# A gated MLP on one core: the first products taken per block of 128 tokens as each is turned, the second weight in two loads of whole rows, one sum of x in a tile of its own

## The chip, the cores and the metric

The kernel runs on one core of a Trainium2 chip. The metric is the device time of one execution in microseconds (us), the median of several runs. Below, PE is the matrix engine (a weight load and a matmul are two instructions of it), DVE, ACT and POOL are the vector, scalar and GpSimd engines, SP is the engine that only issues transfers here. Each engine works through its own queue in order; semaphores tie the queues together.

## The reference

```python
batch, seq, dim, hidden = 16, 256, 512, 2048   # x, w1 (dim x 2*hidden), w2 (hidden x dim), float32
h = x @ w1
gate, value = np.split(h, 2, axis=-1)
h = np.maximum(gate, 0) * value
return (h @ w2).astype(np.float32)
```

So there are 4096 tokens of 512 numbers; the first product makes 2 x 2048 numbers of each (a gate and a value), the second brings 2048 back to 512.

## The kernel before

**Tiling.** The tokens go in four sweeps `s` of 1024, each two halves of 512. A sweep has 16 hidden blocks `jb` of 128; after the last one, the second product of the sweep runs as a stream of 128 steps that interleaves with the next sweep's first blocks. Both products take seven multiplications where a plain 2 x 2 block product takes eight. For the first one the 2 x 2 blocks of x are A11, A12 (first half of the tokens, first and second 256 of dim) and A21, A22 (second half); those of w1 are B11, B12, B21, B22 (rows of dim by gate and value). Sums T1..T4 of weight blocks (T1 = B12 - B11, T2 = B22 - T1, T3 = B22 - B12, T4 = B21 - T2) and S1..S4 of x blocks (S1 = A21 + A22, S2 = S1 - A11, S4 = A12 - S2, S3 = A11 - A21) are made first. A block's seven products are called P1 (B11, A11), P2 (B21, A12), P3 (B22, S4), P4 (T4, A22), P5 (T1, S1), P6 (T2, S2), P7 (T3, S3); each is two matmuls of 512 columns, 14 in all. Between them ACT copies X to Y after P1 (L252; P2 waits for it, since it adds into X), makes scaled copies after P5 and P6 (L259, L266), and DVE joins the parts (L272, L273, L278, L288). The second product does the same with g (the gated result) and w2: its sums are L165 on g (into `w_stage`) and T1..T4 on w2's tiles (`vop`).

**The weights' way in.** w1 arrives in nine pieces `wl`: hidden blocks 0 and 1 alone, then seven pairs (2,3) .. (14,15). A load of a piece is two transfers on SP's queue, gate columns and value columns (L212, 256 KB each for the single blocks, in rows of 512 bytes; 512 KB each for the pairs), into six slots of `w_stage`; a slot is loaded again only when ACT has copied its B11, B21, B22 (L231, `copy_some`) and POOL has made its T1..T4 (L227, `sum_w1`). The fifth piece (blocks 6, 7) goes into the slots of blocks 0 and 1, the sixth (8, 9) into those of (2, 3). w2 arrives by POOL's own queue, in float16, in four transfers of 512 KB (L668), each issued between two pieces' sums. When the last piece is done, POOL issues the casts of x for the next sweeps (L192) and then makes w2's T1 and T2 (L670, L671, 128 x 2048 each).

**The start.** The T's need both halves of a piece, and S's need the second half of the tokens, so hidden blocks 0 and 1 of sweep 0 are computed by the plain way, eight products (`Plain`, L314): a gate and a value, each four matmuls, per token half. x arrives in eight blocks of 128 tokens (L475) and is turned by PE (L485; the first four from float32, the last four from float16 after a cast by POOL or DVE, L478), DVE and ACT copying the turned halves out of PSUM (L488). Fillers that compute nothing (`arm`, `keep_busy`, L502 and L150) stand between. The order of every engine's queue is the order in which the code is written: SP first x blocks 0 and 1, the gate columns of w1's block 0, x blocks 2 and 3, its value columns, both transfers of block 1, then x blocks 4 to 7 and the first pairs. PE: x blocks 0 and 1 turned; fillers; block 0's gate on 256 tokens; x blocks 2 and 3 turned; fillers; its gate on the other 256; its value; block 1's gate and value; then x blocks 4 to 7 turned among the same for the second half. Copies of block 0's and 1's weights to float16 (`plain_w`): three on POOL (L455), one on ACT (L456). The seven-product blocks begin with block 2; its P1 stands before the last piece of block 1's value.

**The second product's sums.** `SUMS_FIRST` and the lines under `if s == 0` say at which step of the stream DVE is given each sum; an emission at step u stands in DVE's queue before what step u itself gives it. In `SUMS_FIRST` each bracket is a token block t with the steps of its S1, S2, S4, S3.

Of the kernel before, what the change touches and what calls it, by code (L numbers as in the profile page):

```python
# [96 lines left out]
def fast_way(ctx, tc, x2, w1, w2, out2, flag):  # L97
# [27 lines left out]


    w1_v = w1.rearrange("(e p) (g j) -> g p e j", p=P, g=2)
    w2_v = w2.rearrange("(u hc p) (v n) -> u v p hc n", u=2, v=2, p=P)
    out_v = out2.rearrange("(s h b p) n -> s h b p n", p=P, h=2, b=NB // 2)

    wop = {n: wpool.tile([P, 2, H], F16, name=f"w_{n}") for n in ("B11", "B21", "B22", "T1", "T2", "T3", "T4")}
    vop = {n: wpool.tile([P, NJ // 2, DO // 2], F16, name=f"v_{n}") for n in ("B11", "B21", "B22", "T1", "T2", "T3", "T4")}
    w_stage = wpool.tile([P, 6, 1024], F32, name="w_stage")
    g_set = {0: gpool.tile([P, NJ, 2 * TH], F16, name="g", tag="g")}

# [11 lines left out]
    def keep_busy(n):  # L147

        for _ in range(n):
            nc.tensor.matmul(Y[:, :TH // 2], warm_b[:, :P], warm_b[:, :TH // 2], start=False, stop=True,  # L150
                             skip_group_check=True)
# [29 lines left out]
    def look_whole(t, at, of, half=False):  # L181

        sq = tmp.tile([P, 1024], F16, name="sq", tag="sq", bufs=1)
        nc.scalar.activation(sq[:, :of], t, SQUARE, scale=(P / of / (2 if half else 1)) ** 0.5,
                             accum_out=st[:, at:at + 1])

    x16 = {}
# [21 lines left out]
    def load_w1(eng, jb, n, u, vs=(0, 1)):  # L209
        t = w_stage[:, u:u + n].rearrange("p u v -> p (u v)").rearrange("p (g e j) -> p g e j", g=2, e=4)  # L210
        for v in vs:
            eng.dma_start(out=t[:, v], in_=w1_v[v, :, :, jb * P:(jb + n) * P])  # L212
        return t.rearrange("p g (k b) j -> p k b g j", k=2)
# [23 lines left out]

    class Block:
        def __init__(self, xo, g, jb):
            self.xo, self.g, self.jb = xo, g, jb  # L240

        def mm(self, name, ps, fresh):
            wn, xn = WX[name]
# [24 lines left out]
        def P3(self):  # L268
            self.mm("P3", self.W, False)
            cc = tmp.tile([P, 2, TH], F32, name="cc", tag="tmp")  # L270
            self.c12, self.c22 = cc[:, 0], cc[:, 1]
            nc.vector.scalar_tensor_tensor(out=self.c12, in0=self.W, scalar=GS, in1=self.u2, op0=MULT, op1=ADD)  # L272
            nc.vector.scalar_tensor_tensor(out=self.g[:, self.jb, :TH], in0=self.X, scalar=0.0,  # L273
                                           in1=self.c12, op0=MAX, op1=MULT)

        def P7(self):
            self.mm("P7", self.Y, False)
            nc.vector.scalar_tensor_tensor(out=self.c22, in0=self.Y, scalar=GS, in1=self.p5, op0=MULT, op1=ADD)  # L278
            second_halves()

        def P4(self):
# [11 lines left out]
    def second_halves():  # L293

        while later:
            later.pop(0).second_half()
# [129 lines left out]
    def fetch(i, eng):  # L426
        if i < len(wl):
            assert all(j > i - 3 for j, _ in copies)
            jb, n, u = wl[i]
            ws[i] = load_w1(eng, jb, n, u)  # L430
# [16 lines left out]
            c()  # L447
        del copies[:n]

    def plain_w(i):  # L450
        jb, n, _ = wl[i]
        t = ws.pop(i)
        js = slice(jb * P, (jb + n) * P)
        for n, k, v in (("B11", 0, 0), ("B21", 1, 0), ("T3", 0, 1)):
            nc.gpsimd.tensor_copy(out=wop[n][:, :, js], in_=t[:, k, :, v])  # L455
        return lambda: nc.scalar.copy(out=wop["B22"][:, :, js], in_=t[:, 1, :, 1])  # L456

    def plain_w_end(jb, n, i):
        n2, i0, i1 = (("T1", "T3", "B11"), ("T2", "B22", "T1"), ("T3", "B22", "T3"), ("T4", "B21", "T2"))[i]
# [17 lines left out]
    def cast_first(b, copy):  # L477
        copy(out=x16_first[b // 2][:, b % 2], in_=xn[1][b])  # L478
# [15 lines left out]
    def new_w():  # L494
        return psw.tile([P, TH], F32, name="W", tag="W")
# [4 lines left out]
    def arm(ps):  # L500

        nc.tensor.matmul(ps, warm_b[:, :P], warm_b[:, :TH], start=True, stop=True)  # L502

    dve, act, pool = nc.vector.tensor_copy, nc.scalar.copy, nc.gpsimd.tensor_copy
    fetch_first(0, (0, 1))
    ws[0] = load_w1(nc.sync, *wl[0], (0,))
    fetch_first(0, (2, 3))
    load_w1(nc.sync, *wl[0], (1,))
    fetch(1, nc.sync)
    make_identity(nc, ident)  # L510
    fetch_first(1, range(4))
    fetch(2, nc.sync)
# [4 lines left out]
    first_half, second_half = (xo["A11"], xo["A12"]), (xo["A21"], xo["A22"])  # L517
    YS = [new_y(), new_y()]

    def halves(*ts):  # L520
        return [t[:, :2 * P] for t in ts]

    def turns(t):
        return [t.bitcast(F16)[:, c:c + 2 * P] for c in (0, 2 * P)]

    rest = plain_w(0)
    turn_first(xo, 0, 0, halves(*YS), (dve, act))
    XS = [new_x(), new_x()]
    turn_first(xo, 0, 1, halves(*XS), (dve, act))
    arm(YS[0])  # L530
    arm(YS[1])
    keep_busy(3)
    plain[0].open(W=False)
    plain[0].part("gate", *first_half, half)
    turn_first(xo, 0, 2, halves(*XS), (dve, act))
    turn_first(xo, 0, 3, halves(new_w(), new_w()), (dve, act))
    keep_busy(2)
    plain[0].part("gate", *first_half, other)
    plain[0].W = new_w()
    rest()  # L540
    rest = plain_w(1)
    plain[0].part("value", *first_half)
    plain[0].value()
    plain[1].open()
    plain[1].part("gate", *first_half)
    rest()
    fetch(4, nc.sync)
    plain[0].gate(0)
    plain[1].part("value", *first_half)
    spare = plain[0].X, plain[1].W  # L550
    cast_first(0, pool)
    cast_first(1, dve)
    cast_first(2, pool)
    turn_first(xo, 1, 0, (turns(YS[0])[0], turns(YS[1])[0]), (dve, act))
    turn_first(xo, 1, 1, (turns(plain[0].X)[0], turns(plain[0].W)[0]), (dve, act))
    plain[1].value()
    held = plain[1].held(0)
    cast_first(3, dve)
    xo["S3"] = halfs.tile([P, 8, P], F16, name="xh", tag="xh").rearrange("p (a b) c -> p a (b c)", a=2)
    sums = [sums_of({n: t[:, :, slice(*c)] for n, t in xo.items()}) for c in (half, other)]  # L560
    next(sums[0])
    plain[0].open()
    plain[0].part("gate", *second_half, half)
    turn_first(xo, 1, 2, turns(spare[0]), (act, act))
    turn_first(xo, 1, 3, turns(spare[1]), (dve, dve))
    plain[0].part("value", *second_half, half)
    plain[1].open(*reversed(YS))
    plain[1].part("gate", *second_half, half)
    plain[1].part("value", *second_half, half)
    next(sums[1])  # L570
    next(sums[0])
    next(sums[1])
    plain[0].part("gate", *second_half, other)
    plain[0].part("value", *second_half, other)
    for n in ("S4", "S3"):
        sum_of(xo, n)
    held()
    prepare(2, False)
    sum_w1(6)
    copy_some(1)  # L580
    plain[0].value()
    copy_some(1)
    plain[1].part("gate", *second_half, other, False)
    prepare(3, False)
    w_sums[:4] = [w_sums[i] for i in (2, 0, 3, 1)]
    sum_w1()
# [5 lines left out]

    def last_plain_out():
        plain[1].value()
        plain[0].gate(1)
        plain[1].gate(1)

    LOOKX, looks = {}, []

# [11 lines left out]

    def look_w2(i):
        n = ("B11", "B21", "B22", "T1")[i // 2]
        look_whole(vop[n].rearrange("p (u h) n -> p u (h n)", u=2)[:, i % 2], NX + 16 + i, 1024, n == "T1")

    def judge():
        n = st.shape[1]
# [23 lines left out]
    TAIL = 4  # L641
    CASTS = {(0, 11): 1, (0, 14): 2, (1, 8): 3, (2, 3): 0}
    SUMS = (10, 11, 12, 13)
    SUMS_FIRST = (10, 11, 13, 45), (17, 22, 26, 53), (33, 37, 41, 66), (67, 72, 76, 80)
    SUMS_AT = (10, 11, 13, 15), (22, 26, 30, 36), (46, 53, 57, 61), (70, 78, 82, 87)
    for s in range(NS):
        if s not in g_set:
# [8 lines left out]
        for at in range(first * PERIOD, (NJ - 1) * PERIOD + 14):  # L656
# [3 lines left out]
            if at in plan:  # L660
                jb, n = plan[at]
                if s == 0 and n == "P5" and jb % 2 == 0:
                    todo += 1
                    if todo < len(wl):
                        prepare(todo)
                    if 5 <= todo < 9:
                        n2 = ("B11", "T3", "B22", "B21")[todo - 5]
                        nc.gpsimd.dma_start(out=vop[n2], in_=w2_v[(0, 0, 1, 1)[todo - 5], (0, 1, 1, 0)[todo - 5]])  # L668
                if (s, n, jb) == (0, "P7", 13):
                    nc.gpsimd.tensor_tensor(vop["T1"], vop["T3"], vop["B11"], op=SUB)  # L670
                    nc.gpsimd.tensor_tensor(vop["T2"], vop["B22"], vop["T1"], op=SUB)  # L671
                if n == "P1" and jb == (14 if s == 0 else 2) and s + 1 < NS:
                    xo_next = x_tiles()
                    load_x(s + 1, xo_next)
# [12 lines left out]
                if s == 0 and (n, jb) == ("P5", NPLAIN):  # L687
                    last_plain_out()
                if n == "P7" or (n, jb) == ("P5", NPLAIN + 1) or n == "P6" and (s, jb) != (0, NPLAIN):
                    copy_some(1)  # L690
                if s == 0 and n == "P7" and jb % 2:
                    fetch(jb // 2 + 5, nc.sync)
                if n == "P6" and (s, jb) in LOOKX:
# [12 lines left out]
            for u in at:  # L706
                job(u, lambda sums=sums: next(sums))
        if s == 0:
            for n2, i0, i1, at in (("T3", "B22", "T3", (46, 50)), ("T4", "B21", "T2", (57, 64))):
                for i, u in enumerate(at):  # L710
                    part = [vop[n][:, i * NJ // 4:(i + 1) * NJ // 4] for n in (n2, i0, i1)]
                    job(u, lambda part=part: nc.vector.tensor_tensor(*part, op=SUB))
            for i, u in enumerate((74, 78, 82, 83)):
                job(u, lambda i=i: plain_w_end(0, NPLAIN, i))
        if s + 1 < NS:
# [16 lines left out]
            job(90, lambda: tc.mark_branch_hint_location("general", "LikelyTaken", [ENG.PE, ENG.DVE, ENG.SP]))  # L732
            advance(stream, 112, jobs)
        prev = stream
    return verdict[1]
# [1 line left out]
_INS = ['x', 'w1', 'w2']  # L737
_OUTS = [((16, 256, 512), 'float32')]
# [25 lines left out]
```

## Time and profile before

| | us |
|---|---|
| median of 5 runs (310.17 to 311.2) | 310.22 |
| the profiled execution | 310.39 |
| its span in the trace | 308.6 |
| PE busy | 301.5 (98%), 1863 matmuls |
| DVE / ACT / POOL busy | 236.0 / 176.8 / 154.5 |
| granted TensorE clock, each of 40 slices | 0.9 or more of full |

The span is what the trace covers; 1.8 us lie around it. Busy times are shares of the whole span and say little of any one stage. A busy PE is counted up to a matmul's modelled end, which lies after the start of the next one; starts are the sharper reading. Where 512-column matmuls follow each other without a wait, two of them start 0.43 us after the two before (0.216 us each), and eight of 256 columns take 0.87 us (0.109 each): a start later than that is a wait, even where the busy time shows none.

### The profile page before, as it was taken

To read this page: it belongs to the slowest core of one execution; us is meant where nothing else is said; L and a number is where in the kernel's file an instruction comes from. 1 tells how busy PE (TensorE), PEld (TensorE's weight loads), DVE (VectorE), ACT (ScalarE), POOL (GpSimd) and SP (SyncE) were. 2 spreads that over 40 slices of the span, in tenths; PEclk is the share of its full clock that TensorE was granted. 3 is DMA by queue.
4 is the path that set the end of the run, shared out by engine and by line. 5 is a ranking of instruction groups with operands and counts; after the bars stand their busy time and mean duration, and the time that the engine had idled before them with its cause. 6 is when DMAs were issued, how large, how long until landed. Compare 5 with 4: busy or idle time off the path is not lost.

```text
span 308.6 us, 5215 instructions
## 1 busy us (share of the span) xinstructions
PE 301.5 (98%) x1863; PEld 181.6 (59%) x1863; DVE 236.0 (76%) x383; ACT 176.8 (57%) x350; POOL 154.5 (50%) x192
## 2 busy tenths in 40 slices
PE   7999999999999999999999999999999999999994
PEld 4554444588854444478864444458884444447883
DVE  1589888889778888887538888888536888888841
ACT  2588985445865555537855555545866555553231
POOL 1389999930058999400028968910006998700000
PEclk9999999999999999999999999999999999999999
DMA  6985798984684233001356910000325110001132
GB/s 201 353 264 189 225 233 105 166 182 80 207 255 100 73 69 68 2 0 36 136 179 112 189 66 4 0 0 4 134 101 173 35 36 0 1 3 34 53 118 74
DMA packets 37917, 32.87 MB, mean 106 GB/s; under 512 B 14465, under 2 KB 33409, under 8 KB 37761
## 3 DMA queue, kind: packets, MB, share of 16 engines
q1 hardware_dynamic: 33536, 26.22, 28.1%
q0 software_dynamic: 4352, 6.29, 12.0%
q8 instruction: 15, 0.25, 0.3%
q14 instruction: 14, 0.11, 0.1%
HBM read 27.26 MB, written 12.58 MB: 129 GB/s over the span
## 4 chain that ended last, share of the span: by engine, by line
PE 88%; DMA 6%; POOL 3%; DVE 1%; SPq 1%; issue 1%; ACT 0%; DVEq 0%; POOLq 0%
PE Y L245 24%; PE X L245 16%; PE W L245 16%; PE Y L351 14%; PE W L351 9%; PE X L351 8%; DMA w_stage<-in_w_dram 6%; POOL w_T L227 3%; SPq L475 1%; DVE w_stage L165 1%; DVE g L288 0%; ACT Y L252 0%; SPq L212 0%; ACT o L394 0%; PE X L630 0%
## 5 line engine op out<-in xcount | busy, mean ns | idle before, releaser
L245 PEld LDWEIGHTS <-w_T 128*128 128x128 f16 x496 | 48.5, 98 | 56.8 <-POOL w_T L227 0.3
L175 POOL TENSOR_TENSOR fold<-xh 128x1024 f32<-128x1024 f16 x16 | 30.3, 1894 | 92.3 <-DMA xh<-x 91.5
L245 PE MATMUL X<-x_A,w_B 128*128 128x512 f16 x248 | 73.7, 379 | 0.1
L245 PE MATMUL Y<-x_S,w_T 128*128 128x512 f16 x220 | 65.4, 379 | 0.0
L245 PEld LDWEIGHTS <-w_B 128*128 128x128 f16 x372 | 36.4, 98 | 42.4 <-issue 0.9
L272 DVE SCALAR_TENSOR_TENSOR cc<-W,pu 128x512 f32<-128x512 f32 x62 | 42.8, 691 | 20.3 <-ACT pu L266 20.3
L252 ACT COPY Y<-X 128x512 f32<-128x512 f32 x62 | 35.4, 570 | 38.0 <-PE X L245 37.7
L266 ACT ACTIVATE pu<-Y 128x512 f32<-128x512 f32 x62 | 37.0, 597 | 33.8 <-PE Y L245 32.8
L178 POOL TENSOR_TENSOR fold<-fold 128x512 f32<-128x512 f32 (+2 forms) x96 | 51.7, 539 | 7.5
L351 PEld LDWEIGHTS <-w_stage 128*128 128x128 f16 x512 | 49.8, 98 | 6.6 <-DVE w_stage L165 0.8
L278 DVE SCALAR_TENSOR_TENSOR cc<-Y,pu 128x512 f32<-128x512 f32 x62 | 42.8, 691 | 6.7
L273 DVE SCALAR_TENSOR_TENSOR g<-X,cc 128x512 f16<-128x512 f32 x62 | 42.9, 691 | 2.3
L288 DVE SCALAR_TENSOR_TENSOR g<-Y,cc 128x512 f16<-128x512 f32 x62 | 42.2, 681 | 1.8 <-PE Y L245 1.8
L351 PEld LDWEIGHTS <-g 128*128 128x128 f16 x384 | 37.6, 98 | 8.2
L259 ACT ACTIVATE pu<-W 128x512 f32<-128x512 f32 x62 | 37.2, 599 | 0.2 <-ACT Y L252 0.2
L245 PE MATMUL W<-x_S,w_B 128*128 128x512 f16 x124 | 36.9, 379 | 0.0
L245 PE MATMUL W<-x_S,w_T 128*128 128x512 f16 x124 | 36.9, 379 | 0.0
L245 PE MATMUL Y<-x_A,w_T 128*128 128x512 f16 x124 | 36.9, 379 | 0.0
L351 PE MATMUL Y<-v_T,w_stage 128*128 128x256 f16 x256 | 33.2, 273 | 0.0
L351 PE MATMUL X<-v_B,g 128*128 128x256 f16 x256 | 31.9, 273 | 0.0
L165 DVE TENSOR_TENSOR w_stage<-g 128x1024 f16<-128x1024 f16 x32 | 22.2, 710 | 0.2
L383 DVE SCALAR_TENSOR_TENSOR o<-W,pu 128x256 f32<-128x256 f32 x16 | 6.7, 422 | 18.4 <-PE W L351 18.4
(103 smaller groups left out, 289.5 us busy)
## 6 DMA issues: line engine op xcount, KB each, us to landing
w_stage<-in_w_dram SPq DMA_DIRECT2D x14, 512.0 KB, 5.9
out_dram<-o SPq DMA_DIRECT2D x26, 256.0 KB, 2.0
x<-in_x_dram POOLq DMA_DIRECT2D x4, 1024.0 KB, 9.2
xh<-x SPq DMA_DIRECT2D x16, 256.0 KB, 3.4
v_B<-in_w_dram POOLq DMA_DIRECT2D x3, 512.0 KB, 6.4
out_dram<-o SPq DMA_DIRECT2D x12, 128.0 KB, 1.7
w_stage<-in_w_dram SPq DMA_DIRECT2D x4, 256.0 KB, 6.0
x_S<-in_x_dram SPq DMA_DIRECT2D x4, 256.0 KB, 5.9
```

What stands on the lines that cost most here:

```text
L165: eng.tensor_tensor(o[n], o[i0], o[i1], op=op)
L175: nc.gpsimd.tensor_tensor(fold, t, t, op=MULT)
L178: nc.gpsimd.tensor_tensor(fold[:, :, :m], fold[:, :, :m], fold[:, :, m:2 * m], op=ADD)
L245: nc.tensor.matmul(ps, wop[wn][:, b, self.jb * P:(self.jb + 1) * P], self.xo[xn][:, b, :], start=fresh and b == 0, stop=b == 1, skip_group ...
L252: nc.scalar.copy(out=self.Y, in_=self.X)
L259: nc.scalar.activation(self.p5, self.W, COPY, scale=GS)
L266: nc.scalar.activation(self.u2, self.Y, COPY, scale=GS)
L272: nc.vector.scalar_tensor_tensor(out=self.c12, in0=self.W, scalar=GS, in1=self.u2, op0=MULT, op1=ADD)
L273: nc.vector.scalar_tensor_tensor(out=self.g[:, self.jb, :TH], in0=self.X, scalar=0.0, in1=self.c12, op0=MAX, op1=MULT)
L278: nc.vector.scalar_tensor_tensor(out=self.c22, in0=self.Y, scalar=GS, in1=self.p5, op0=MULT, op1=ADD)
L288: nc.vector.scalar_tensor_tensor(out=self.g[:, self.jb, TH:], in0=self.Y, scalar=0.0, in1=self.c22, op0=MAX, op1=MULT)
L351: nc.tensor.matmul(ps, self.op[an][:, i], vop[wn][:, i], start=name in ("P1", "P5") and i == 0, stop=i == NJ // 2 - 1, skip_group_check=True)
```

## The change

- SP's queue: both transfers of w1's block 0 stand before x blocks 2 and 3, both of block 1 behind them.
- `plain_w` takes one transfer at a time: its first matrix is copied by POOL, its second by DVE; ACT has none.
- Block 0's gate and value on the first 256 tokens come as soon as they can, and then both for x block 2 and for x block 3 alone (matmuls of 128 columns); block 0's second half does so for each of its four x blocks. Block 1 stays at 512 and 256 columns. Fillers are five, as before, and lie elsewhere. x block 4 is cast by DVE, 5 to 7 by POOL.
- S3 of sweep 0 lies in the tile `sq` (the scratch of ACT's later look at the weights) and no longer in a third `xh` buffer; the sums of the first 256 tokens and the last 256 are each made over 256 columns, S4 over all.
- In the seven-product block 2, DVE makes block 1's last g and block 2's own first g (`behind`) after P7's part and no longer before.
- At P6 of block 5 ACT no longer copies if the copy would be of the sixth w1 piece (8, 9); that copy comes one place later.
- w2 comes in two transfers of 1024 KB (whole rows: 512 numbers in place of 256), issued when the seventh and eighth pieces' sums are made, and the four former `vop` tiles are views of two row tiles.
- w2's T2: first half on POOL, second half on DVE at step 12. T4's second half at step 62 (64 before), S3 of t = 2 at step 64 (66 before).
- `look_w2` reads its piece as 4 x 256 and no longer as one row of 1024; the last value returned is `verdict[-1]`.

```diff
-    vop = {n: wpool.tile([P, NJ // 2, DO // 2], F16, name=f"v_{n}") for n in ("B11", "B21", "B22", "T1", "T2", "T3", "T4")}
+    vop = {n: wpool.tile([P, NJ // 2, DO // 2], F16, name=f"v_{n}") for n in ("T1", "T2", "T4")}
+    w2_rows = [wpool.tile([P, NJ // 2, DO], F16, name=f"w2_{u}") for u in range(2)]
+    vop.update({n: w2_rows[u][:, :, v * DO // 2:(v + 1) * DO // 2]
+                for n, u, v in (("B11", 0, 0), ("T3", 0, 1), ("B21", 1, 0), ("B22", 1, 1))})
...
+            if not self.behind:
+                self.first_half()
+
+        def first_half(self):
             nc.vector.scalar_tensor_tensor(out=self.g[:, self.jb, :TH], in0=self.X, scalar=0.0,
                                            in1=self.c12, op0=MAX, op1=MULT)
...
+            for job in self.behind:
+                job()
             second_halves()
...
+    def plain_w(i, v, engines):
+
+        (jb, n, _), t = wl[i], first_w[i]
         js = slice(jb * P, (jb + n) * P)
+        for k, (n, copy) in enumerate(zip((("B11", "B21"), ("T3", "B22"))[v], engines)):
+            copy(out=wop[n][:, :, js], in_=t[:, k, :, v])
+
+    def sum_w2(eng, n2, i0, i1, i):
+        eng.tensor_tensor(*[vop[n][:, i * NJ // 4:(i + 1) * NJ // 4] for n in (n2, i0, i1)], op=SUB)
...
     fetch_first(0, (0, 1))
-    ws[0] = load_w1(nc.sync, *wl[0], (0,))
+    first_w = [load_w1(nc.sync, *wl[0])]
     fetch_first(0, (2, 3))
-    load_w1(nc.sync, *wl[0], (1,))
-    fetch(1, nc.sync)
+    first_w.append(load_w1(nc.sync, *wl[1]))
...
+    plain_w(0, 0, (pool, dve))
     arm(YS[0])
     arm(YS[1])
+    plain[0].open()
+    plain[0].part("gate", *first_half, cols(0, 2))
+    plain_w(0, 1, (pool, dve))
+    keep_busy(4)
+    plain[0].part("value", *first_half, cols(0, 2))
+    turn_first(xo, 0, 2, halves(*XS, c=2 * P), (dve, act))
+    keep_busy(1)
+    turn_first(xo, 0, 3, halves(*YS, c=2 * P), (dve, act))
+    plain_w(1, 0, (pool, dve))
+    plain_w(1, 1, (pool, dve))
+    for b in (2, 3):
+        for which in ("gate", "value"):
+            plain[0].part(which, *first_half, cols(b), False)
+    fetch(4, nc.sync)
     plain[0].value()
     plain[1].open()
     plain[1].part("gate", *first_half)
+    cast_first(0, dve)
+    cast_first(1, pool)
+    cast_first(2, pool)
+    cast_first(3, pool)
+    plain[1].part("value", *first_half, half)
+    turn_first(xo, 1, 0, (turns(YS[0])[0], turns(YS[1])[0]), (dve, act))
     plain[0].gate(0)
+    plain[1].part("value", *first_half, other, False)
...
+    for which in ("gate", "value"):
+        plain[0].part(which, *second_half, cols(0))
+    turn_first(xo, 1, 1, (turns(YS[0])[1], turns(YS[1])[1]), (dve, act))
+    turn_first(xo, 1, 2, (turns(spare[0])[0], turns(spare[1])[0]), (dve, act))
+    xo["S3"] = tmp.tile([P, 1024], F16, name="sq", tag="sq", bufs=1).rearrange("p (a b) -> p a b", a=2)
...
+    turn_first(xo, 1, 3, (turns(spare[0])[1], turns(spare[1])[1]), (dve, act))
...
+        blocks[NPLAIN].behind = (plain[1].held(1), blocks[NPLAIN].first_half)
...
-    SUMS_FIRST = (10, 11, 13, 45), (17, 22, 26, 53), (33, 37, 41, 66), (67, 72, 76, 80)
+    SUMS_FIRST = (10, 11, 13, 45), (17, 22, 26, 53), (33, 37, 41, 64), (67, 72, 76, 80)
...
-                    if 5 <= todo < 9:
-                        n2 = ("B11", "T3", "B22", "B21")[todo - 5]
-                        nc.gpsimd.dma_start(out=vop[n2], in_=w2_v[(0, 0, 1, 1)[todo - 5], (0, 1, 1, 0)[todo - 5]])
+                    if todo in (6, 7):
+                        nc.gpsimd.dma_start(out=w2_rows[todo - 6], in_=w2_v[todo - 6])
                 if (s, n, jb) == (0, "P7", 13):
                     nc.gpsimd.tensor_tensor(vop["T1"], vop["T3"], vop["B11"], op=SUB)
-                    nc.gpsimd.tensor_tensor(vop["T2"], vop["B22"], vop["T1"], op=SUB)
+                    sum_w2(nc.gpsimd, "T2", "B22", "T1", 0)
...
-                    copy_some(1)
+                    copy_some(0 if (s, n, jb) == (0, "P6", 5) and copies[0][0] == 5 else 1)
...
-            for n2, i0, i1, at in (("T3", "B22", "T3", (46, 50)), ("T4", "B21", "T2", (57, 64))):
+            for n2, i0, i1, at in (("T3", "B22", "T3", (46, 50)), ("T4", "B21", "T2", (57, 62))):
...
+            job(12, lambda: sum_w2(nc.vector, "T2", "B22", "T1", 1))
```

## The prediction

> **What bounds the kernel now.** First the stretches of the run, engine by engine (us, then busy us and count of PE, PEld, DVE, ACT, POOL):
>
> ```profile
> 4.24:6.98 2.74, 2.16 (x15) 1.62 (x13) 0.85 (x2) 0.74 (x2) 0.46 (x2) 1.00 0.78 241
> 6.98:17.75 10.77, 10.34 (x81) 6.87 (x82) 6.31 (x15) 5.55 (x14) 4.05 (x9) 1.00 1.10 351
> 17.75:31.00 13.25, 13.12 (x61) 5.67 (x59) 11.30 (x18) 12.11 (x24) 13.17 (x15) 1.00 0.65 206
> 31.00:62.00 31.00, 31.00 (x155) 14.97 (x154) 27.21 (x42) 21.66 (x40) 30.52 (x25) 1.00 0.94 183
> 62.00:66.00 4.00, 3.76 (x33) 2.94 (x32) 3.33 (x5) 1.48 (x4) 2.45 (x1) 1.00 0.85 180
> 66.00:84.00 18.00, 18.00 (x165) 15.84 (x164) 15.72 (x30) 12.60 (x29) 0.00 (x0) 1.00 0.56 137
> 84.00:302.00 218.00, 218.00 (x1342) 130.89 (x1340) 169.95 (x272) 120.98 (x238) 103.15 (x138) 1.00 0.26 72
> ```
>
> From 84 on PE never stops and the change leaves that work alone, so what PE gains or loses before 84 is gained or lost at the end, one for one. Up to 17.75 the transfers are full (share 1.10, 351 GB/s), and from 17.75 to 62 POOL is nearly as full as PE. So I read the waits of PE one by one, from starts in the timeline:
>
> ```profile
> 14.03 0.40 PE L485 MATMUL W<-ident,xh 128*128 128x128 f16 x4
> 14.26 0.38 PE L314 MATMUL W<-x_S,w_T 128*128 128x256 f16 x2
> ...
> 16.67 0.86 POOL L227 TENSOR_TENSOR w_T<-w_stage 128x256 f16<-128x256 f32 x1 [3.17 <-DMA w_stage<-in_w_dram]
> 16.86 1.22 DVE L165 TENSOR_TENSOR xh<-x_A,x_S 128x1024 f16<-128x1024 f16 x1
> 17.75 0.59 PE L245 MATMUL W<-x_S,w_T 128*128 128x512 f16 x2
> 18.29 0.59 PE L245 MATMUL X<-x_A,w_B 128*128 128x512 f16 x2
> 18.71 0.59 PE L245 MATMUL Y<-x_S,w_T 128*128 128x512 f16 x2
> 19.32 0.59 PE L245 MATMUL W<-x_S,w_B 128*128 128x512 f16 x2
> ...
> 29.35 0.62 ACT L231 CAST w_B<-w_stage 128x512 f16<-128x512 f32 x1 [0.49 <-DMA w_stage<-in_w_dram]
> 29.79 0.59 PE L245 MATMUL Y<-xh,w_T 128*128 128x512 f16 x2
> 29.87 0.58 ACT L252 COPY Y<-X 128x512 f32<-128x512 f32 x1
> 30.50 0.59 PE L245 MATMUL X<-x_A,w_B 128*128 128x512 f16 x2
> ...
> 60.38 4.07 POOL L671 TENSOR_TENSOR v_T<-v_B,v_T 128x2048 f16<-128x2048 f16 x1
> 62.47 2.35 PE L351 MATMUL X<-v_B,g 128*128 128x256 f16 x20
> 63.45 1.55 DVE L165 TENSOR_TENSOR w_stage<-g 128x1024 f16<-128x1024 f16 x1
> 65.06 1.05 PE L351 MATMUL W<-v_T,w_stage 128*128 128x256 f16 x8 [0.24 <-DVE w_stage L165]
> 65.09 0.69 DVE L165 TENSOR_TENSOR w_stage<-w_stage,g 128x1024 f16<-128x1024 f16 x1
> 76.56 1.05 PE L351 MATMUL Y<-v_T,w_stage 128*128 128x256 f16 x8
> ```
>
> With 0.43 for two 512-column matmuls the waits are 0.11 before 18.29 (17.75 + 0.43 = 18.18), 0.18 before 19.32, 0.11 before 22.46 (P4 of block 2, after a start at 21.92), 0.28 before 30.50. That last one is ACT's: its queue holds the copy of piece (8, 9), which landed at 29.3, ahead of the X-to-Y copy that P2 of block 6 needs. In the second product 20 x 0.109 from 62.47 ends at 64.65, so 0.41 is lost before 65.06: DVE's S1 took 1.55 where its equals take 0.69, while POOL's T2 ran to 64.45. Then 0.14 before 76.56 (the row before starts 75.55, + 0.87) and 0.06 before 77.49. Together 1.29 us: this is all there is to win behind 17.75.
>
> **The start, term by term.** Transfers land in the order of issue (issue + time to landing): x block 1 at 4.1, block 0's gate 6.5, x 2 and 3 at 7.4 and 8.1, block 0's value 9.0, block 1's two at 9.9 and 10.8, x 4 at 11.4, then 0.7 each to 13.5, pair (2, 3) at 15.0 and 16.5. The change swaps 0.9 (value) with 0.7 + 0.7 (two x blocks): value at 7.4, x 2 and 3 at 8.3 and 9.0, the rest as before. PE then: gate on 256 tokens 6.98 (4 x 0.109), four fillers, value 7.87 to 8.30, x 2 turned from 8.34 (0.43), a filler, x 3 from 9.06, blocks 2 and 3 at 128 columns (16 pairs x 0.058) to 10.5. Block 1's gate could start at 10.43 before, when its copy was done; so the early value buys nothing here. Gate to 11.4, half a value to 11.8; x block 4, landed 11.4, DVE's cast of 0.43, turned at 12.07. From there, counted with the copies' delays (0.32 DVE, 0.43 ACT after the turn, then 0.29 and 0.37), PE has value 0.43, 32 pairs 1.86, three turns 0.7, gate 0.87, half value 0.43, P1 0.43, half value 0.43 = 5.15, and some 0.6 of waits for turned blocks: P5 of block 2 at **17.83** against 17.75. T1, on POOL from 16.67 to 17.53, is still there in time. So the rearranged front is worth +0.08, since x's last blocks and pair (2, 3) land no sooner.
>
> *128-column pairs*, 48 new ones in place of 24 at 256: 0.23/4 = 0.058 each by the turns at 14.03 against 0.054 of a longer one; bound above by a weight load that hides nothing, 98 ns (mean of the PEld groups), +1.9 in all; below 0.054, nothing. I take 0.058, the same form. *Rule:* the Trainium skill, "TensorE: Matmul & The Clock Gate", section "Back-to-back issue gap", gives about 81 ns for a sustained load-and-matmul pair at 128 columns, counting both. By it the front would be 48 x 0.023 = 1.1 us longer and the whole gain gone; the 16 turns of this trace run at 58, so I go by them.
>
> *Transfers*, not shown before: two 512-byte-row loads back to back while the queue is still starting. The first took 2.4 after x 1 (4.1 to 6.5), later ones 0.9. If the second takes 2.4 too, all landings are 1.5 later; if it fills the slack of the first, they could be 0.3 sooner. Nearer to 0.9, since x 2 behind the first took 0.9 and x 3 0.7; I take **+0.15**, all on the path.
>
> *Copies by DVE beside POOL's* (four pairs, POOL 0.40; DVE between 0.2 and the 0.43 of its 512-wide cast). *Rule:* "SBUF — State Buffer", section "Who interferes with whom": a DVE copy in a two-port mode, or one with two SBUF inputs, and a POOL instruction exclude each other for a whole instruction. The rows at 16.67 and 16.86 agree for sums (0.86 for POOL's 0.72, 1.22 for DVE's 0.69), none shows it for casts; by the rule each pair would be 0.2 to 0.4 later. By the rows, if a pair goes one after the other, block 0's value still waits for its own landing at 7.4 and block 1's gate starts at 10.7 for 10.5, covered by the wait for x block 4 at 12.07. I cost it at nothing; without that cover 0.2 to 0.4.
>
> *ACT after P5.* ACT has no weight copies and makes v of block 0 earlier; its copies after P1 and P5 then stand right behind PE, so P3 starts at 19.23, not 19.32: of the two waits 0.17 goes, net **-0.09** with the +0.08. *DVE's order at block 2* brings the part that P4 waits for to 21.8, from 22.41: **-0.11**; the two g's it pushes back are read at 59, but DVE is then late by one part at block 3: **+0.06** (0.69 each, 2.76 a block against PE's 3.02, so it catches up). *ACT's skipped copy*: **-0.28**; piece (8, 9) has its first use at 35.25, two blocks later, and POOL's T1 for block 6 is done at 28.5 against its use at 29.36, so nothing of POOL stops an earlier PE. *S3's own tile*: the scratch is next written at 68, S3 last read at 60.3: nothing.
>
> **w2.** Four POOL issues (1.08, 0.93, 0.91, 0.91) become two, so POOL is 1.9 earlier by 54: T1 from 54.2 (56.22 before) to 58.3, half of T2 (2.04) to 60.4. The two loads are issued at about 41.7 and 48.4. Half-size ones took 5.9 to 9.0; twice the bytes in equally many pieces is between 5.9 and 15, and x's cast, as many bytes, landed 4.9 behind the one before it: I take 8, so 50 and 56.4, before the first use at 59. B21 used to land at 60.66. Then S1 finds POOL idle: 0.69 from 63.45, before PE asks at 64.65: **-0.41**. T2's second half costs DVE 0.68 between S2 and S4; S2 ends 64.9, T2 65.6, S4 66.3, wanted at 66.4 and 67.3. If the second load lands after 61.4, POOL still runs beside S1 and the 0.41 stays. Steps 62 and 64 put S3 one DVE instruction (0.68) earlier: **-0.20** for the waits of 0.14 and 0.06. The x casts go out 1.9 earlier too, so SP's turning transfers (65.64 on) and the stores behind them start sooner, never later. `look_w2` and the returned verdict: the same instructions, nothing.
>
> Sum: +0.15 - 0.09 - 0.11 + 0.06 - 0.28 - 0.41 - 0.20 = -0.88. The profiled execution took 310.39 (span 308.6), 0.17 above the median: 309.5 there, **309.3** as a median.
>
> **Rivals.** (1) *The start's transfers slip*: 0.8 to 1.5 us more on every landing to 16.5, POOL's T's with them, eats the gain: 310.0 to 310.7. For it: 2.4 us for one such load; against: 0.9 for the three that come later. (2) *The lock stays* since w2 lands late: 309.7 (310.22 - 0.47). Against: x's cast. (3) *Pairs of 128 columns run at the weight load's 98 ns*: +1.9 in place of 0, so 311.2, slower; it decides from 58 + 0.88/48 = 76 ns a pair on. Against: the turns, and weights loaded ahead in every row. (4) *The second load fills the idle transfers at 4 to 6*: 0.3 sooner, 308.9.
>
> **How the numbers follow.** Forecast 0.62, rivals 0.11, 0.12, 0.07, 0.08. No change is within 0.2%, 309.60 to 310.84, which is about what a measurement of this kernel can tell: faster takes nearly all of the forecast, rival 4 and a little of rival 2 (0.71); same is rivals 1 and 2 with the forecast's edge (0.19); slower rival 3 and the worst of 1 (0.10). Range 308.7 (rival 4, with 0.2 to spare) to 310.3 (rival 1 in its lower half); the forecast alone 308.9 to 309.7.
>
> **What would show it.** P5 of block 2 within 0.3 of 17.8; x block 4 landed by 11.7; 128-column pairs at 58 ns; no wait before P2 of block 6; S1 on g at 0.69 us and PE unbroken from 62 to 84. Wrong if x block 4 lands after 12.3, if pairs run at 76 ns or more, if S1 still takes over a microsecond, or if a new wait stands where POOL's sums meet a PE that is now ahead.

## The result and the profile after

| | kernel before | changed kernel |
|---|---|---|
| median, us | 310.61 (61 runs, 309.65 to 311.51) | 310.12 (36 runs, 308.45 to 311.61) |
| profiled execution, us | 310.39 | 310.56 |
| its span, us | 308.6 | 308.7 |

The ratio of the medians is 0.9982 with a 95% interval of 0.9973 to 0.9990: about 0.5 us faster where 0.9 was forecast, inside the 0.2% that I had called no change. The forecast of 309.3 was counted from 310.22, the median of five runs; 61 runs put the kernel before at 310.61, so of the 0.8 us between 309.3 and 310.12 some 0.4 lies in that base. Five of the changed kernel's 36 runs took 308.45 to 308.59 us and the rest 309.24 or more; none of the five was profiled, so why they were shorter is open. The two profiled executions show no gain at all. So the question is where it went.

First the stretches of the changed kernel, in the cuts of before (us, then busy us and count of PE, PEld, DVE, ACT, POOL):

```profile
17.75:31.00 13.25, 13.12 (x63) 5.87 (x61) 10.65 (x17) 11.86 (x23) 13.09 (x15) 1.00 0.65 206
62.00:66.00 4.00, 4.00 (x37) 3.47 (x36) 3.37 (x6) 1.87 (x5) 0.00 (x0) 1.00 0.88 190
66.00:84.00 18.00, 18.00 (x165) 15.99 (x164) 15.68 (x31) 12.85 (x29) 0.00 (x0) 1.00 0.61 145
```

POOL is idle from 62 (2.45 us busy there before) and PE loses nothing from 62 to 84. Then the timeline of the changed kernel at the places that the prediction named, and at the two ends of sweep 1:

```profile
16.80 1.29 POOL L231 TENSOR_TENSOR w_T<-w_stage 128x256 f16<-128x256 f32 x1 [2.50 <-DMA w_stage<-in_w_dram]
16.81 0.68 DVE L168 TENSOR_TENSOR x_S<-x_A,x_S 128x1024 f16<-128x1024 f16 x1
...
18.14 0.60 PE L249 MATMUL W<-x_S,w_T 128*128 128x512 f16 x2
...
30.26 0.59 PE L249 MATMUL X<-x_A,w_B 128*128 128x512 f16 x2
...
59.63 2.13 POOL L468 TENSOR_TENSOR v_T<-w,v_T 128x1024 f16<-128x1024 f16 x1 [0.89 <-DMA w<-in_w_dram]
...
62.23 2.35 PE L361 MATMUL X<-w,g 128*128 128x256 f16 x20
...
63.21 0.69 DVE L168 TENSOR_TENSOR w_stage<-g 128x1024 f16<-128x1024 f16 x1
...
64.42 1.04 PE L361 MATMUL W<-v_T,w_stage 128*128 128x256 f16 x8
...
83.66 0.59 PE L249 MATMUL X<-x_A,w_B 128*128 128x512 f16 x2
...
302.31 1.04 PE L361 MATMUL Y<-v_T,g 128*128 128x256 f16 x8
```

and the last two of these in the kernel before:

```profile
84.50 0.59 PE L245 MATMUL X<-x_A,w_B 128*128 128x512 f16 x2
...
303.15 1.04 PE L351 MATMUL Y<-v_T,g 128*128 128x256 f16 x8
```

P2 of block 6 starts without a wait (30.26; 29.83 + 0.43), S1 on g takes 0.69, the first P5 of the second product starts at 64.42 where it was 65.06. PE enters sweep 1 0.84 us earlier and is still 0.84 earlier at its last group. Yet the span ends no sooner: from the start of PE's last group to the end of the span it is 5.46 us before (308.61 - 303.15) and 6.38 after (308.69 - 302.31). I call this stretch **the end**. What lies in it is the last output store. The transfers issued from 303.7 in the changed kernel, and then those from 304.5 in the kernel before (issue, KB, us from issue to landing; q8 and q14 are instruction fetches):

```profile
q8 instruction: 1, 0.02, 1.4%
q14 instruction: 2, 0.02, 1.1%
...
out_dram<-o SPq DMA_DIRECT2D x1, 128.0 KB, 3.2
```

```profile
q14 instruction: 2, 0.02, 1.4%
...
out_dram<-o SPq DMA_DIRECT2D x1, 128.0 KB, 2.3
```

The same 128 KB take 3.2 us in place of 2.3, and the changed kernel has a 16 KB fetch of instructions (q8, from 304.74) begun after the store's issue at 303.79; the kernel before had its own at 304.28, begun ahead of the store (304.63). Of the store's 16 parts the trace of the changed kernel has 15 landed by 305.69 and one at 307.04; SP waits for that one, and the span ends 1.65 us behind it.

### The profile page after: what moved, and what is told of

It reads as the page before. It is cut to its first block, busy times and chain, and to the rows that moved or that the text cites. A ratio compares the mean times of both kernels' runs of the same rounds, so it can differ in the third digit from the quotient of the medians.

```text
span 308.7 us, 5258 instructions
## 1 busy us (share of the span) xinstructions
PE 300.5 (97%) x1891; PEld 183.0 (59%) x1891; DVE 236.0 (76%) x388; ACT 176.5 (57%) x348; POOL 151.5 (49%) x189
## 4 chain that ended last, share of the span: by engine, by line
PE 92%; DMA 4%; SPq 1%; POOL 0%; issue 0%; ACT 0%; POOLq 0%
PE Y L249 26%; PE W L249 17%; PE X L249 17%; PE Y L361 14%; PE W L361 9%; PE X L361 9%; DMA w_stage<-in_w_dram 2%; DMA x_S<-in_x_dram 2%; SPq L487 0%; POOL w_T L231 0%; SPq L216 0%; ACT o L404 0%; PE X L650 0%; SPq L778 0%; POOLq L231 0%
## 5 line engine op out<-in xcount | busy, mean ns | idle before, releaser
L361 PE MATMUL X<-w,g 128*128 128x256 f16 x256 | 31.9, 273 | 0.0
L168 DVE TENSOR_TENSOR w_stage<-g 128x1024 f16<-128x1024 f16 x32 | 21.4, 683 | 0.2
L231 POOL TENSOR_TENSOR w_T<-w_stage 128x512 f16<-128x512 f32 (+1 forms) x16 | 18.7, 1175 | 2.5 <-DMA w_stage<-in_w_dram 2.5
```

What stands on the lines that cost most here:

```text
L168: eng.tensor_tensor(o[n], o[i0], o[i1], op=op)
L361: nc.tensor.matmul(ps, self.op[an][:, i], vop[wn][:, i], start=name in ("P1", "P5") and i == 0, stop=i == NJ // 2 - 1, skip_group_check=True)
```

## The experiments

In all of them I read three stretches of the profile: from the landing of x block 4 to P5 of block 2; from there to the first P1 of sweep 1 (the two before sum to "the body"); and the end. From the first P1 of sweep 1 to PE's last group it was 218.65 us in all 18 profiles, so nothing is won or lost there.

**1. Both kernels without the general way.** If the branch and its code fetches hold the last store, the end must shrink without them.

```
-    with tc.If(unfit > 0, label="general"):
-        with ExitStack() as general:
-            general_way(general, tc, x2, w1, w2, out2)
...
-            job(90, lambda: tc.mark_branch_hint_location("general", "LikelyTaken", [ENG.PE, ENG.DVE, ENG.SP]))
```

> The kernel before without the general way and its branch at the end (for these inputs it is never taken; the verdict is still computed and loaded). Theory T (tail): what the change gained in TensorE time is lost, in part and at random, in the landing of the last output store, which shares the DMA rings with the instruction fetches around the end branch. Then the last store lands 1.4 to 1.8 us after its issue (2.27 with the branch), PE's last group still starts near 303.15, and the time falls by 0.5 to 1 us, to 309.4 to 310. Rival N (the landing varies by itself, the branch has nothing to do with it): the last store takes 2 us or more, the time stays at 310.3 to 310.6 or moves by the branch's own 0.3 at most.

> The changed kernel without the general way and its branch. Theory T: the last store lands 1.4 to 1.8 after its issue (3.25 with the branch), PE's last group starts near 302.3, the time is 308.6 to 309.1, and the difference to the kernel before without the branch is the 0.84 that PE shows, not the 0.5 measured with the branch. Rival N: the last store takes over 2 us in some runs, the difference between the two stays near 0.5. Rival S (what varies is the start of the transfers, and the change's extra early loads cost more there than PE's clock shows): the difference stays near 0.5 with both tails short.

308.70 (308.38 to 309.09) and 307.25 us (306.85 to 307.78), six runs each, beside 310.36 for the kernel before on that chip. The end is 4.16 and 4.14 us, every one of the last three stores lands in 1.7, and no fetch lies in it. From 303 on in the changed kernel without the branch:

```profile
q1 hardware_dynamic: 288, 0.26, 26.7%
...
out_dram<-o SPq DMA_DIRECT2D x1, 128.0 KB, 1.7
```

So the branch costs the kernel before 1.9 us and the changed one 2.9 (310.61 - 308.70, 310.12 - 307.25). Without it the change is worth 1.45 us. The six runs of each lie within 0.7 to 0.9 us, the 61 and 36 with the branch within 1.9 and 3.2; with so unequal counts that does not show the branch to be the cause of the scatter. Theory T holds in its mechanism: with the branch the end is 1.3 to 2.8 us longer, by an amount that differs from kernel to kernel. In every profile the end has three parts: 1.48 us from the start of PE's last group to the issue of the last store; the store, 1.70 and 1.72 without the branch and 2.27 to 3.86 with it; and what follows its landing, 0.96 without and 1.65 to 1.71 with. So between kernels with the branch it is the store that differs. The times themselves fell below both forecasts (309.4 to 310 and 308.6 to 309.1), and the 1.45 is more than the 0.84 expected.

**2. What the rearranged front is worth.** The kernel before up to block 2, the rest from the change.

```
-                    if 5 <= todo < 9:
...
+                    if todo in (6, 7):
+                        nc.gpsimd.dma_start(out=w2_rows[todo - 6], in_=w2_v[todo - 6])
...
+                    copy_some(0 if (s, n, jb) == (0, "P6", 5) and copies[0][0] == 5 else 1)
```

> The kernel before up to block 2, with the rest of the change: w2 in two loads, T2 in halves, the two steps moved, ACT's copy skipped. Theory: the rearranged front is worth nothing (predicted +0.08 at block 2's P5 and +0.15 of transfers, less 0.09 and 0.11), so this kernel's PE is as far ahead at the end as the changed one: P2 of block 6 without a wait, S1 at 0.69 us, first P1 of sweep 1 at 83.6 to 83.75 (84.50 before, 83.66 after). Rival F (the front brings some of the 0.84): 83.8 to 84.0.

309.41 us, ratio 0.9967 (0.9953 to 0.9981). My absolute times could not be used, since x block 4 landed at 11.07 in this execution and at 11.48 and 11.60 in the two that I had; counted from P5 of block 2, sweep 1 starts 65.88 us later, against 66.75 before and 65.52 or 65.63 after. So w2 and the skipped copy are worth 0.87 us, and the front 0.25 to 0.36 behind P5. Its body is 72.12, the changed kernel's 72.06. The theory, that the front is worth about nothing, stands for the body; but this kernel's end is 5.75, near that of before. By one profile of each, that is 0.63 of the 0.71 us by which it beats the changed kernel.

**3. The sum that came late at block 2.**

```
+        if m < n:
+            w_sums[0] = lambda: step(*steps[0], eng=nc.vector)
...
+    prepare(2, False)
+    sum_w1(1)
     sum_of(xo, "S4")
     held()
-    prepare(2, False)
-    sum_w1(6)
+    sum_w1(5)
```

> The changed kernel with the first T1 of block 2 taken by DVE ahead of its S4 sum, in place of POOL beside it (there it took 1.28 us, blocked by S4, and P5 of block 2 waited for it until 18.14). Theory: the lock is what is late, so T1 is done by 17.1 to 17.3, P5 of block 2 starts at 17.8 to 17.9, and PE keeps 0.15 to 0.3 of it to the end: first P1 of sweep 1 at 83.4 to 83.5. Rival: POOL's T2 then meets S4 in its place and P6 of block 2 (18.99 after) waits, or S4 is late for P3 (19.45): nothing is kept, 83.6 to 83.7.

309.82 us. P5 of block 2 stands 6.22 behind x block 4's landing, where the changed kernel has 6.54: T1 on DVE takes 0.42, and 0.3 is won, of which 0.1 goes again (65.63 for 65.52 behind P5). In the changed kernel without the branch POOL began T1 0.03 us ahead of S4, and then it was DVE that waited:

```profile
16.38 0.73 POOL L228 TENSOR_TENSOR w_T<-w_stage 128x256 f16<-128x256 f32 x1 [2.49 <-DMA w_stage<-in_w_dram]
16.41 1.24 DVE L165 TENSOR_TENSOR x_S<-x_A,x_S 128x1024 f16<-128x1024 f16 x1
...
17.43 0.60 PE L246 MATMUL W<-x_S,w_T 128*128 128x512 f16 x2
```

There T1 was in time, P5 6.26 behind the landing. Hundredths of a microsecond decide 0.28 us: S4 blocked T1 in eight of the nine profiles that have both engines at it in this order, in three of them though T1's recorded start was ahead of S4's, by 0.004 to 0.02 us; in the ninth it was 0.03 ahead.

**4. Two terms by themselves.** The skipped copy put back, and T2 whole on POOL again; one execution of each, so only the stretches of its profile count.

```
-                    copy_some(0 if (s, n, jb) == (0, "P6", 5) and copies[0][0] == 5 else 1)
+                    copy_some(1)
```

```
-                    sum_w2(nc.gpsimd, "T2", "B22", "T1", 0)
+                    nc.gpsimd.tensor_tensor(vop["T2"], vop["B22"], vop["T1"], op=SUB)
...
-            job(12, lambda: sum_w2(nc.vector, "T2", "B22", "T1", 1))
```

> The changed kernel with ACT's skipped weight copy put back in its old place. Theory: the wait ahead of P2 of block 6 is back (0.2 to 0.3 us), and from P5 of block 2 to the first P1 of sweep 1 PE takes 65.8 to 65.9 us (65.52 after, 65.63 without the branch). Rival: DVE or POOL is late there anyway and it stays at 65.5 to 65.65.

> The changed kernel with w2's T2 taken whole on POOL again. Theory: POOL then ends near 64 (59.6 plus 4.1 plus its wait for the load), S1 on g runs 1.5 us beside it, PE loses 0.3 to 0.4 before the first P5 of the second product, and P5 of block 2 to first P1 of sweep 1 takes 65.9 to 66.0. Rival: S1 is done in time all the same, 65.5 to 65.65.

The copy costs more than expected: 66.09 for 65.52, that is 0.57. ACT took the copy of the piece just landed, and PE's P2 stood behind the X-to-Y copy after it:

```profile
28.71 0.62 ACT L235 CAST w_B<-w_stage 128x512 f16<-128x512 f32 x1 [0.78 <-DMA w_stage<-in_w_dram]
28.86 0.59 PE L249 MATMUL Y<-sq,w_T 128*128 128x512 f16 x2
...
29.23 0.58 ACT L256 COPY Y<-X 128x512 f32<-128x512 f32 x1
...
29.86 0.59 PE L249 MATMUL X<-x_A,w_B 128*128 128x512 f16 x2 [0.40 <-ACT Y L256]
```

T2 whole costs nothing here, 65.52 as before the edit; this expectation missed:

```profile
57.65 4.07 POOL L690 TENSOR_TENSOR v_T<-w,v_T 128x2048 f16<-128x2048 f16 x1
...
62.06 0.69 DVE L168 TENSOR_TENSOR w_stage<-g 128x1024 f16<-128x1024 f16 x1
```

POOL is done at 61.7, ahead of S1, because it has two issues fewer and here w2's second load landed at 56.94. Where it landed at 59.49, as in the changed kernel's profile, T2 whole would have run to 63.7, into S1 at 63.21; that was not tried.

**5. Where PE's code stands.** In every trace 16 KB of code are fetched (queue q8) after some 250 PE instructions, by the mean over a trace, so I take these fetches for PE's, a block of 256 instructions each. The change adds 56 PE instructions (28 weight loads, 28 matmuls), and the last such fetch moves from 226 PE instructions ahead of the branch's own fetch (at 291.78) to 36 ahead of it (301.31). First the place was moved with more dummy matmuls at the start, 51 and 40 of 128 columns in place of 7 of 512. They leave the other 384 columns of their PSUM bank unset, and the two kernels' outputs are not the reference's; they serve for timing alone.

```
-    for i in range(NWARM):
-        nc.tensor.matmul(Y, warm_b[:, :P], warm_b[:, :TH], start=True, stop=True)
+    for i in range(51):
+        nc.tensor.matmul(Y[:, :P], warm_b[:, :P], warm_b[:, :P], start=True, stop=True)
```

> The changed kernel with its 7 opening dummy matmuls of 512 columns replaced by 51 of 128 (about the same 3 us of TensorE at the start, 88 more instructions), so that the fetch of PE's next 256 instructions, which came at 301.31, 36 instructions ahead of the branch at the end, comes about 4.8 us earlier. Theory P (page): that fetch just ahead of the end holds back the branch's own fetch (304.74 after, 2.43 us behind the start of PE's last group, against 1.13 before), so the last store lands late; with the page moved, the branch's fetch starts about 1.1 us after the last group's start, the end (span less the start of PE's last group) takes 5.4 to 5.8 us in place of 6.4, and the time is 309.1 to 309.5 (310.12 after). Rival L (the longer code or plain chance, not the page's place): end still 6 us or more, time 309.9 to 310.3.

> The kernel before with its 7 opening dummy matmuls replaced by 40 of 128 columns (66 more PE instructions), which puts the boundary of PE's 256 instructions as close ahead of the end as the changed kernel has it. Theory P: a 16 KB fetch at about 1 us before PE's last group, the branch's fetch 2.4 us behind that group's start, an end of 6.4 us in place of 5.45, time 311.2 to 311.6. Rival L: end 5.4 to 5.8, time 310.3 to 310.7.

The ends are 5.84 and 6.77: each kernel took on about the other's end. The kernel before came to 311.39 for 310.57 (ratio 1.0017, 1.0000 to 1.0034, hardly clear of noise), and 0.33 of that lies at P5 of block 2, which stands 6.60 behind x block 4's landing for 6.27. The changed one came to 309.7 only, since the 51 took 5.59 us, a fetch at 14.28 put the second load of pair (2, 3) at 17.27, and P5 of block 2 came 7.60 behind x block 4's landing, a microsecond late. So the place was then set with every instruction the same, by an alignment ahead of PE's code:

```
+    nc.tensor.addr_align(256, offset=20, max_nops=0)
     with _tile.TileContext(nc) as tc:
```

> The changed kernel, every instruction the same, with PE's code laid so that its first instruction stands in slot 20 of a block of 256; counted from there the branch at the end stands some 215 slots into its block (36 instructions behind a fetch in the changed kernel, 226 in the kernel before). Theory P (page): no fetch of PE's next block in the last 10 us, PE's branch takes 0.4 us in place of 1.6, the branch's fetch starts 1.2 to 1.4 us behind the start of the branch in place of 2.5, the end (span less the start of PE's last group) is 5.4 to 5.9 us, and the time 309.2 to 309.6. Rival L (code length, chance): end 6.3 to 7, time as the changed kernel's 310.1.

> The control: the changed kernel with PE's first instruction in slot 100, which puts the branch some 40 slots into its block, as it is without any laying out. Theory P: fetch 1 us ahead of PE's last group, branch 1.6 us, end 6.3 to 7, time 309.9 to 310.4; about 0.8 longer than with slot 20. Rival L: the same time and end as with slot 20.

> The kernel before with PE's first instruction in slot 157, which puts its branch some 40 slots into its block. Theory P: PE's branch takes 1.6 us, end 6.3 to 7 in place of 5.46, time 311.2 to 311.6 against 310.5. Rival L: 310.3 to 310.7.

> The changed kernel with the first T1 of block 2 on DVE ahead of S4 and PE's code laid as with slot 20. Theory: both losses gone, P5 of block 2 6.2 us behind x block 4's landing (6.54 after), the end 5.4 to 5.9, time 308.9 to 309.3, faster than both kernels. Rival: one of the two comes back elsewhere, 309.4 or more.

With slot 20 the end is 5.73 and, with T1 on DVE, 5.77, as theory P has it. I had taken the changed kernel's own first slot for 100; by the counts it is 100 - (79 - 36) = 57, so slots 100 and 157 put the branch not 40 but 79 and 77 instructions behind the fetch. The two ends that I expected to be long came out at 6.08 and 5.94, and the two kernels are no controls but two more points: 309.21 us for slot 100, 310.85 for the kernel before with slot 157 (its profiled execution, 312.03, is the longest of eleven). The times with slot 20, 310.70 and 310.25, missed by about a microsecond. What it won at the end it paid at the start: a fetch at 1.88 us lay among the first loads, x block 0 landed at 4.75 for 3.48, and x block 4 at 11.82 and 11.85 where the other eleven profiles of the new order have 10.97 on average. The median of slot 20 is another 0.6 above its profiled execution (310.12), which this does not explain. The fetch among the transfers from 1 to 4 us:

```profile
q8 instruction: 1, 0.02, 3.1%
```

Whether the end alone gives the gain back was still open, so four more ran.

> The changed kernel with PE's first instruction in slot 200, which puts the branch some 180 slots behind the last fetch (36 in the changed kernel, 244 with slot 20, 79 with slot 100). Theory P: PE's branch 0.4 us, end 5.4 to 5.9, x block 4 landed by 11.6 (11.8 with slot 20), time 309.0 to 309.4 against 310.12 of the changed kernel. Rival C (slot 100 was chance): 309.9 or more.

> The same kernel as with slot 100, a second time. Theory P: 309.0 to 309.5, end 5.9 to 6.2. Rival C: 309.8 to 310.2.

> Slot 100 and the first T1 of block 2 on DVE ahead of S4. Theory: P5 of block 2 6.2 us behind x block 4's landing (6.5 where S4 blocks T1), end 5.9 to 6.2, time 308.8 to 309.2. Rival: no gain over slot 100 alone.

> Slot 200 and the first T1 of block 2 on DVE. Theory: as with slot 200, less 0.2 to 0.3: 308.7 to 309.1, the fastest of all with the branch. Rival: the same as slot 200 alone.

Slot 200 gives the end forecast for it (5.55, 5.59), but its times, 309.92 and 309.78 us, miss the forecasts of 309.0 to 309.4 and 308.7 to 309.1; they are what rival C said. The front loses it: beside its fetches at 10.00 and 11.74 x block 5 landed 1.42 behind block 4, and block 7 1.42 behind block 6, where 0.7 is usual, and P5 of block 2 stands 7.17 and 6.87 behind x block 4, in place of 6.54 and 6.22. Slot 100 stood a second time, 309.39 for 309.21, with its fetch at 15. In its two profiles the end gives 0.30 and 0.58 us of that; x block 4 landed at 10.60 and 10.48, 1.0 and 1.1 ahead of the changed kernel's profile, so how much of the 0.7 to 0.9 is the end's is not separated. With T1 on DVE besides it has the lowest median of the kernels with the branch, **309.09 us** (six runs), ratio to the kernel before 0.9949 (0.9935 to 0.9964). Slot 100 alone has 0.9951 (0.9935 to 0.9966): that T1 on DVE adds to it is not shown. All ends together, from the trace's records:

| PE instructions from the last block fetch to the branch's fetch | kernels | PE's branch, us | the end, us |
|---|---|---|---|
| 28 to 36 | changed kernel, t1_vector, copy_back, t2_whole, before_page | 1.62 to 1.96 | 6.38, 6.44, 6.99, 6.81, 6.77 |
| 77 to 82 | after_slot100 twice, t1_slot100, before_slot157 | 0.40 to 0.49 | 6.08, 5.80, 5.71, 5.94 |
| 120 to 245 | before, front_before, after_page, after_slot20, t1_slot20, after_slot200, t1_slot200 | 0.39 to 0.41 | 5.46, 5.75, 5.84, 5.73, 5.77, 5.55, 5.59 |
| no branch | before_no_branch, after_no_branch | | 4.16, 4.14 |

## Why the prediction was wrong

**The step that failed** is the sentence "From 84 on PE never stops and the change leaves that work alone, so what PE gains or loses before 84 is gained or lost at the end, one for one." Its first half held to the hundredth (218.65). But the sum then took the stretch behind PE's last group for a constant, and the change lengthened it by 0.92 us. No term stood for the 56 new PE instructions other than their time on PE. They moved a block fetch to 36 instructions ahead of the branch's own fetch; PE's branch then takes 1.62 us for 0.40, its 16 KB fetch comes 2.54 us behind the start of the branch in place of 1.24, and so 0.95 us after the last store's issue and no longer 0.35 ahead of it. In the two profiles the account closes: -0.96 in the body, +0.12 in the landing of x block 4 and +0.92 in the end are the +0.08 of the spans. In the medians the branch costs 0.96 us more than before (2.87 for 1.91), about the end's 0.92, and leaves 0.49 of the 1.45. That the fetch's place decides the end is shown in the changed kernel by moving it and nothing else (6.38 at 36 instructions, 5.55 to 6.08 at 79 to 244); to lengthen the end of the kernel before, instructions were added. Why a block fetch close ahead makes PE's branch 1.2 us longer is not shown.

The Trainium skill, "Runtime: NRT & Kernel Launch", section "Instruction fetch mechanics", has the block of 256 instructions in 16 KiB, which the traces bear out, and says that crossing into a new block is mostly hidden and that a taken branch out of the window forces a fetch. The fetch behind every closing branch here agrees with the second. As to the first, the crossings between the first P1 of sweep 1 and PE's last group leave no mark, 218.65 us in all 18 profiles; but one beside a transfer that something waits for was not hidden, 0.92 us at the end and 0.63 to 0.65 in the front with slot 200.

**The body was right.** The terms without the transfers' 0.15 sum to -1.03; measured it is -0.96 (73.02 to 72.06) where S4 blocks T1 and -1.13 (71.89) where it does not.

- w2, the two steps and the skipped copy: -0.89 predicted, -0.87 measured. The shares are other than I said. By t2_whole, one execution, the 0.41 comes without T2's split, from the two POOL issues saved, at least where the load lands early; the copy is worth 0.57 in the changed kernel, where I took 0.28 from its wait in the kernel before.
- w2's second load: 56.4 predicted; from 56.94 to 59.61 in the traces. 8 us was too little, 11.7 in the profile after. It decided nothing, as T2 still ended before S1.
- "T1, on POOL from 16.67 to 17.53, is still there in time" was wrong in most executions: 1.29 us, and P5 of block 2 at 18.14. The prediction had priced this very lock for the casts and not for T1 beside S4, though the row at 16.86 had it. It costs 0.28.
- The copies by DVE beside POOL cost nothing, as said: the gate of block 0 starts at 7.59 for 6.98, 0.49 of it because its load landed at 6.96 for 6.47, and the wait for x block 4 takes it up. Beside each other a POOL and a DVE copy took 0.40 and 0.48 us, the next two 0.52 and 0.29 (from 10.14 and 10.95).
- 128-column pairs at 58 ns held, so rival 3 fell. By the 81 ns of the Trainium skill ("TensorE: Matmul & The Clock Gate", section "Back-to-back issue gap") the 48 pairs would, by estimate, have cost 1.1 us more; the body, shorter by 0.96, does not agree.
- Transfers +0.15: 11.60 for 11.48 in the two profiles. But this landing lies anywhere from 10.44 to 11.63 whichever order is used (mean 11.19 in five executions of the old order, 10.97 in eleven of the new, slot 20 left out). Neither the term nor rival 1 is shown.

What stays open: without the branch the change brings 1.45 us in the medians, and its body accounts for 0.96 to 1.13. The landings of the start scatter by more than the rest, but that they make it up is not shown: in the one profile of each without the branch x block 4 lands at 10.95 before and 11.17 after, and the spans differ by 0.91. With the branch, too, the medians differ by 0.49 where the two profiles show no gain.

## What to carry to other kernels

A gain on the bounding engine is only a gain if the stretch behind its last instruction is left as it was; measure that stretch on both sides as its own term, with its stores and its fetches. Adding instructions to an unrolled engine moves all its later code fetches, and one of them can come to lie beside a transfer that something waits for: at a closing branch, or among the first loads. Where runs of one kernel scatter by more than the effect, find the stretches that scatter and compare the rest.

## What the runs showed of the hardware

- A 16 KB instruction fetch took 0.88 to 2.13 us, and a load or store beside it could land late. With a fetch at 13.48 us (before_slot157) the first load of pair (2, 3) landed at 16.52, against 15.02 in the kernel before, whose fetch came at 21.67.
- Matmuls at the start run at half speed. In after_page, from 1.27 on:

```profile
1.27 5.59 PE L148 MATMUL Y<-warm 128*128 128x128 f16 x51 [1.27 <-DVE warm L144]
```

They start 107 ns apart, where matmuls of 128 columns take 58 ns at 14 us; the 7 of 512 in the changed kernel start 427 ns apart, where two take 0.43 us later. The profile shows a granted clock of 1.00 for this stretch, but the trace's clock records begin only at 6.71 us in after_page and 5.07 in the changed kernel (3.9 to 6.9 in the 18 profiles), and time without a record counts as 1.00 in the views. So the 1.00 says nothing of the start, nor does the first slice of the table ahead of the prediction.
- Of a POOL sum and a DVE sum that start within 0.03 us of each other one takes its usual time and the other about that of both: 1.29 (POOL) and 0.68 (DVE) in the changed kernel, 0.73 and 1.24 in the same kernel without the branch.
